# Two gate products of a transformer merge in seven block products of summed operands, with the modulation rows moved into the attention

## The chip, the cores and the metric

One Trainium2 chip, one of its cores. The metric is the device time of one execution in microseconds (us); lower is better. TensorE multiplies matrices into PSUM, VectorE and ScalarE work on elements, GpSimd here only starts accumulating DMAs, SyncE starts most of the loads.

## The reference, cut to what matters

Two layers over 512 latent tokens and 256 context tokens, 1024 channels, all in fp32. Each layer modulates a normalised input, projects it into four branches (A: dense attention, D: windowed attention, B: a Fourier mix, C: a spatial gate) and merges them:

```
def _merge(h, outs, gates, w_br, w_merge, b_merge, w_out):
    yb = jnp.stack([o * jax.nn.silu(z) for o, z in zip(outs, gates)], axis=2)
    y = jnp.einsum('bnrw,rwd->bnrd', yb, w_br)
    g = jax.nn.sigmoid(h @ w_merge + b_merge).reshape(b, n, N_BRANCH, D_MODEL)
    return jnp.sum(g * y, axis=2) @ w_out
```

The gate product `h @ w_merge` is 1024 by 1024 for each branch; the branch product `y` has a depth of 256. The modulation (shift, scale and gate of each layer, for the latent vector `c` and the context vector `c_ctx`) is `silu(c) @ w_ada + b_ada`.

## The kernel before

Everything stands transposed: channels on the 128 partitions (8 tiles `kk`), the 768 tokens in the free dimension, context in columns 0 to 255, latent in 256 to 767. Layer 0 computes all 768 columns, layer 1 the 512 latent ones.

A product keeps fp32 accuracy with two halves of each operand: `hi` is the value rounded to the matmul's type, `lo` the rest, and a product is three matmuls, hi by hi, hi by lo and lo by hi (`mm3`, line 181). The halves of the modulated input are the tiles `hh` and `hl`. Weights come in pieces of 128 x 512 or 128 x 256: `plan` (lines 136 to 151) lists them in the order of use, `wload` (154) starts their loads on SyncE's queue, at most 5 pieces ahead and with 3 buffers, `wround` (162) makes `hi` on ScalarE and `lo` on VectorE, and `wnext` (173) hands out the next piece and rounds up to the piece after it. Each of `hi` and `lo` has 3 buffers.

`merge` (line 645) does one branch in 8 tiles of 128 output channels. A tile takes two pieces of the gate's weights and one of the branch's: for the latent 512 columns and the context's 256 columns the gate product over 8 `kk` (24 matmuls each) and the branch product over 2 (6 each). Then ScalarE's tanh makes the gate (668), VectorE multiplies it with the branch product (670), and the result is added to `M` by a GpSimd DMA (676) or, in the last merge, by VectorE (674), which is followed by the rounding of `M` into `MH` and `ML` (678 to 685). The context columns' bank comes from tag `ctag`; tag "o" has one bank, "t" two, "mm" three.

The written order comes from generators that yield a cost at each step. `drive` (867) runs a main generator and lets a filler or a side generator go on as the costs allow: the attention of A and D is the main one, at a cost per unit of `PACE` (27; 48 units in layer 0), and the filler holds the projections, the merge of C and, once A's attention has ended, the merge of A (931 to 935). What is left of the filler runs after the attention (947). Then come the merge of D and the merge of B, with a side generator at `SIDE` = 0.42 (948 to 957): first `fnet` (781), the Fourier mix that the merge of B needs, then `ada_rest` (247). That one computes 24 rows of the modulation on VectorE (273), two instructions for each half row (`at`), from the vectors in `cb`; its buffers come from tags "z", "sc" and "p". In layer 1 the same with 8 rows and one vector. A planner of the framework then sets the order on each engine: an instruction whose buffer and inputs are ready may go ahead of one that is written before it. Pools have a fixed number of buffers: "k" 10, "z" 4, "yb" 8, "sc" 3, "p" 3, "q" 4.

`Rope.finish` (471) turns queries and keys with the cosine and sine tables `krope`, loaded once (404). `outp` (960) multiplies `MH` and `ML` with the output weights.

## Time and profile before

| | us |
|---|---|
| median of 3 runs | 1202.47 (1201.67 to 1204.15) |
| profiled execution: its own time | 1203.12 |
| its span | 1201.3 |
| TensorE busy / VectorE busy / ScalarE busy | 1180.7 / 734.0 / 472.6 |
| layer 0: attention | 112 to 443 |
| layer 0: last tiles of the merge of A | to 476.1 |
| layer 0: merge of D, first to last branch product | 489.6 to 565.1 |
| layer 0: merge of B, first to last branch product | 575.6 to 648.8 |

The profiled execution's time has 1.8 us around its span. [...]

### The profile page before, as it was taken

The numbers are of one execution on the slowest core, as the hardware profiler recorded it, in microseconds if no ns is written. First come the engines' busy times: TensorE is split into PE (matmuls) and PEld (weight loads), VectorE is DVE, ScalarE is ACT, GpSimd is POOL, SyncE is SP. The second block draws the span as 40 slices with busy tenths as digits, with TensorE's granted clock in tenths as the row PEclk, the third lists the DMA queues.
The fourth block names the chain that finished last, engine by engine and source line by source line (L and its number), as shares of the span: only waits on it lengthen the run. The fifth ranks groups of instructions, "written<-read, shape, count | busy, mean of one in ns | idle before, by whom it ended". The sixth has DMA issues, their size and how long they took to land. (4 is left out here: it accounts for less than half of the span.)

```text
span 1201.3 us, 18858 instructions
## 1 busy us (share of the span) xinstructions
PE 1180.7 (98%) x7164; PEld 1002.3 (83%) x7164; DVE 734.0 (61%) x1567; ACT 472.6 (39%) x935; POOL 14.4 (1%) x20
## 2 busy tenths in 40 slices
PE   6999999999999999999999999999999999999998
PEld 3789888888888888988888888887888888888887
DVE  4683557545565453577886469767756666476553
ACT  5443534433333332322333246545444444333431
POOL 0000000000000000000000000000000000000000
PEclk9999999999999999999999999999999999999999
DMA  7708113212111334567653454462322213355353
GB/s 286 264 17 212 54 45 94 57 36 61 54 45 49 80 79 120 125 180 201 192 163 101 140 161 143 133 170 89 101 63 76 65 57 90 103 171 156 97 171 123
DMA packets 76090, 138.81 MB, mean 116 GB/s; under 512 B 9056, under 2 KB 19424, under 8 KB 76000
## 3 DMA queue, kind: packets, MB, share of 16 engines
q1 hardware_dynamic: 66640, 120.30, 33.8%
q10 hardware_dynamic: 7056, 11.02, 3.1%
q0 software_dynamic: 2304, 6.29, 2.8%
q8 instruction: 56, 0.92, 0.3%
q14 instruction: 34, 0.28, 0.1%
HBM read 115.56 MB, written 4.19 MB: 100 GB/s over the span
## 5 line engine op out<-in xcount | busy, mean ns | idle before, releaser
L169 ACT CAST wh<-wr 128x512 fp32r<-128x512 f32 (+1 forms) x320 | 184.2, 577 | 362.0 <-PE gc L185 95.7
L170 DVE TENSOR_TENSOR wl<-wr,wh 128x512 fp32r<-128x512 f32 (+1 forms) x320 | 202.8, 636 | 191.5 <-ACT wh L169 189.8
L184 PE MATMUL gl<-hh,wh 128*128 128x512 f32 x512 | 204.1, 399 | 0.0
L185 PE MATMUL gl<-hl,wh 128*128 128x512 f32 x512 | 200.2, 391 | 0.0
L187 PE MATMUL gl<-hh,wl 128*128 128x512 f32 x512 | 199.9, 391 | 0.0
L187 PEld LDWEIGHTS gl<-hh,wl 128*128 128x128 f32 x512 | 96.1, 188 | 20.9
L184 PEld LDWEIGHTS gl<-hh,wh 128*128 128x128 f32 x512 | 96.5, 188 | 16.7 <-issue 0.2
L185 PEld LDWEIGHTS gl<-hl,wh 128*128 128x128 f32 x512 | 96.5, 189 | 16.2
L573 DVE TENSOR_REDUCE mx<-s 128x1 f32<-128x768 f32 (+3 forms) x80 | 61.6, 770 | 78.5 <-PE s L567 36.0
L581 ACT ACTIVATE p<-s,ng 128x768 f32<-128x768 f32 (+3 forms) x80 | 60.0, 750 | 102.1 <-DVE ng L578 58.5
L273 DVE CUSTOM_DVE_ANT_0 aj<-at,cb 128x512 f32<-128x512 f32 x112 | 74.2, 688 | 8.3 <-DMA M<-g 4.4
L184 PE MATMUL gc<-hh,wh 128*128 128x256 f32 x256 | 73.5, 287 | 0.0
L187 PE MATMUL gc<-hh,wl 128*128 128x256 f32 x256 | 72.5, 283 | 0.0
L185 PE MATMUL gc<-hl,wh 128*128 128x256 f32 x256 | 72.4, 283 | 0.0
L184 PE MATMUL p<-hh,wh 128*128 128x512 f32 (+1 forms) x192 | 71.2, 371 | 0.0
L184 PE MATMUL ow<-MH,wh 128*128 128x512 f32 (+1 forms) x200 | 69.5, 347 | 1.0 <-DVE xn L972 1.0
L187 PE MATMUL ow<-MH,wl 128*128 128x512 f32 (+1 forms) x200 | 69.4, 347 | 0.8 <-DVE wl L170 0.8
L185 PE MATMUL ow<-ML,wh 128*128 128x512 f32 (+1 forms) x200 | 69.4, 347 | 0.0
L187 PE MATMUL p<-hh,wl 128*128 128x512 f32 (+1 forms) x192 | 68.2, 355 | 0.0
L185 PE MATMUL p<-hl,wh 128*128 128x512 f32 (+1 forms) x192 | 68.2, 355 | 0.0
L668 ACT ACTIVATE g<-gl,bmh 128x512 f32<-128x512 f32 x64 | 43.8, 685 | 60.1 <-PE gl L187 42.0
L597 PE MATMUL tp<-kconst,p 128*128 128x128 f32 x368 | 53.2, 272 | 0.0
(465 smaller groups left out, 2428.3 us busy)
## 6 DMA issues: line engine op xcount, KB each, us to landing
wr<-in_wm_dram SPq DMA_DIRECT2D x128, 256.0 KB, 2.7
wr<-in_win_dram SPq DMA_DIRECT2D x72, 256.0 KB, 2.8
at<-in_wadat_dram SPq DMA_DIRECT2D x64, 256.0 KB, 3.2
wr<-in_wo_dram SPq DMA_DIRECT2D x40, 256.0 KB, 2.9
aw<-in_wada_dram SPq DMA_DIRECT2D x16, 512.0 KB, 5.7
wr<-in_wm_dram SPq DMA_DIRECT2D x64, 128.0 KB, 2.2
ks<-yk SPq DMA_DIRECT2D x32, 192.0 KB, 4.2
M<-g POOLq DMA_DIRECT2D x16, 384.0 KB, 4.9
```

Source lines behind the costliest of these rows:

```text
L169: A.copy(hi[:, :n], raw[:, :n])
L170: V.tensor_sub(lo[:, :n], raw[:, :n], hi[:, :n].bitcast(F32))
L184: T.matmul(d, wh, xh[:, c0:c1], start=first and op, stop=False)
L185: T.matmul(d, wh, xl[:, c0:c1], start=False, stop=False)
L187: T.matmul(d, wl, xh[:, c0:c1], start=False, stop=last and cl)
L273: V.tensor_tensor_reduce(out=junk[:, :512], in0=w[:, :512], in1=cb[2 * v + half][:, :512], scale=0.5, scalar=0.0, op0=ALU.mult, op1=ALU.ad ...
L573: V.reduce_max(out=mx, in_=sv, axis=AX.X)
L581: A.activation(p[:, :nk], sv, AF.Exp, bias=ng, scale=0.125, accum_out=sm_)
L597: T.transpose(tp[:, (i - g0) * P:(i - g0 + 1) * P], p[:, i * P:(i + 1) * P], ident)
L668: A.activation(g[:, q0:q1], gp, AF.Tanh, scale=0.5, bias=bmh[:, r * 8 + j:r * 8 + j + 1])
```

## The change

For the merges of D and B in layer 0 the gate product is done as a product of 2 x 2 blocks with seven block products in place of eight (the scheme of Strassen in Winograd's form). The weights of tiles j and j + 4 make the four blocks (two output tiles by two halves of the depth), and the 768 columns are split in two halves `H1`, `H2` of 384. `merged_s` lists the loads and items of such a round; `prep` makes the sums of weights on VectorE; `combos` makes the sums of columns of `hh` + `hl` and rounds them; `first_sum` puts the rounded first sum into `hh` and `hl` in place; `merge_s` runs the seven blocks and the two branch products of a round, four rounds per merge. Banks `z`, `x`, `y` hold the block products, which are added up partly in PSUM and partly in `g0`, `g1`.

Three tiles of the merge of A (of 8, `HELD` = 5 stay in the filler) are held back until the attention has ended; `fnet` and `combos` are the side work beside them. The rows of the modulation are made one half row per step with a single buffer `row`, and in both layers the steps are laced into the merge of C, `z1`, `b` and the merge of A, one per 4800 units of cost (`ADA`); what is left follows as side work. `cb` and the rope tables share two buffers (tag "rt"), and the tables are loaded again for each use, from ScalarE's queue. `wnext` rounds one piece further ahead, everywhere. Layer 0's pace is 3900.

```diff
-PACE = (4500, 4000)
+PACE = (3900, 4000)
+ADA = 4800
+HELD = 5
...
+        prt = pool("rt", 2)
+        prow = pool("row", 1)
...
+        def merged_s(l, r):
+            def a(j, h):
+                return (wm[l, r, j, :, 512 * h:512 * h + 512], 512, "wraw" if h and j < 4 else "z")
+
+            def y(j):
+                return (wm[l, r, j, :, 1024:], 256)
+
+            first = [load(*a(0, 0)), load(*a(4, 0)), load(*a(4, 1)), load(*a(0, 1))]
+            for j in range(4):
+                a11, a21, a22, a12 = first
+                y0 = load(*y(j))
+                y1 = load(*y(j + 4))
+                if j < 3:
+                    first = [load(*a(j + 1, 0)), load(*a(j + 5, 0)), load(*a(j + 5, 1)), load(*a(j + 1, 1))]
+                s1 = []
+
+                def prep(a11=a11, a12=a12, a21=a21, a22=a22, s1=s1):
+                    t = tl("p", f"s1_{a11}")[:, :512]
+                    V.tensor_add(t, raws[a21], raws[a22])
+                    V.tensor_sub(raws[a21], raws[a11], raws[a21])
+                    V.tensor_sub(raws[a11], t, raws[a11])
+                    V.tensor_sub(raws[a12], raws[a12], raws[a11])
+                    s1.append(t)
+
+                item(a11, 512)
+                item(a12, 512)
+                item(a12, 512, prep, lambda k=a11: raws[k])
+                item(a12, 512, None, lambda k=a21: raws[k])
+                item(a12, 512, None, lambda s1=s1: s1[0])
+                item(y0, 256)
+                item(y0, 512, None, lambda k=a12: raws[k])
+                item(y0, 512, None, lambda k=a22: raws[k])
+                item(y1, 256)
...
+            merged(l, R_A)
+            for r in (R_D, R_B):
+                (merged if l else merged_s)(l, r)
+            outw(l)
...
+            for k in range(len(raws), min(upto, len(loads))):
+                src, n, tag = loads[k]
+                if tag == "z":
+                    raws[k] = tl("z", f"wr{k}")[:, :512]
+                else:
+                    raws[k] = pw.tile([P, 512], F32, name=f"wr{k}", tag="wraw", bufs=W_RAW)
+                nc.sync.dma_start(raws[k][:, :n], src)
...
         def wnext():
 
             i = cnt[0]
             cnt[0] += 1
-            wload(i + LOADS)
+            wload(max(k for k, *_ in items[i:i + LOADS]))
             wround(i + 2)
+            while prepped[0] < min(i + 3, len(items)):
+                prep = items[prepped[0]][2]
+                if prep:
+                    prep()
+                prepped[0] += 1
+            wround(i + 3)
             return ready[i]
...
+            fetch(0)
+            for i, (half, l, j) in enumerate(steps):
+                if i % len(names) == 0:
+                    cb.clear()
+                    for v in range(nv):
+                        t = prt.tile([P, 512], F32, name=f"cb{v}{half}{nv}", tag="rt")
+                        nc.scalar.dma_start(t, crow[v:v + 1, half * 512:half * 512 + 512].to_broadcast([P, 512]))
+                        cb.append(t)
                     yield 1000
+                    for v, t in enumerate(cb):
+                        th = tl("sc", f"cbt{v}{half}{nv}")
+                        A.activation(th[:, :512], t, AF.Tanh, scale=0.5)
+                        V.scalar_tensor_tensor(out=t, in0=th[:, :512], scalar=1.0, in1=t, op0=ALU.add, op1=ALU.mult)
                     yield 1000
-                if j in (7, 15, 23):
+                for v in range(nv):
+                    junk = tl("sc", f"aj{l}_{j}_{half}{v}")
+                    V.tensor_tensor_reduce(
+                        out=junk[:, :512], in0=row[i], in1=cb[v], scale=0.5,
+                        scalar=0.0, op0=ALU.mult, op1=ALU.add, accum_out=macc[j // 16][:, j % 16, v, half:half + 1])
+                fetch(i + 1)
+                yield 1000
...
+            def tables(name):
+                if not TAB:
+                    for i in range(2):
+                        t = prt.tile([P, NL], F32, name=f"rt{i}{name}", tag="rt")
+                        nc.scalar.dma_start(t, krope[:, i * NL:(i + 1) * NL])
+                        TAB.append(t)
+                return TAB
...
+                    cos, sin = tables(name)
                     V.tensor_add(s[:, 0, cs], s[:, 0, cs], s[:, 1, cs])
...
-            def merge(r, first=False, final=False, ctag="mm"):
-                for j in range(KT):
+                for j in part:
...
+            HN = (WC.stop - WC.start) // 2
+            H1, H2 = slice(WC.start, WC.start + HN), slice(WC.start + HN, WC.stop)
+            BO = {}
+            def combos():
+                t23 = [[[tl("k", f"T{n}{part}{i}{l}", F32R) for i in range(2)] for part in "hl"] for n in (2, 3)]
+                t4 = [pq.tile([P, 2, NT], F32R, name=f"T4{part}{l}", tag="q") for part in "hl"]
+                t1 = [tl("k", f"T1{i}{l}") for i in range(2)]
+
+                def at(ts, kk):
+                    return [t[kk // 2][:, (kk % 2) * HN:(kk % 2) * HN + HN] for t in ts]
+
+                for n in (11, 21, 22, 1, 2, 3, 4):
+                    BO[n] = []
+                for kk in range(4):
+                    fa, fb = tl("sc", f"fa{l}{kk}"), tl("p", f"fb{l}{kk}")
+                    for f, k_ in ((fa, kk), (fb, kk + 4)):
+                        V.tensor_add(f[:, WC], hh[k_][:, WC].bitcast(F32), hl[k_][:, WC].bitcast(F32))
+                    one = at([t1], kk)[0]
+                    V.tensor_sub(one, fa[:, H2], fa[:, H1])
+                    V.tensor_sub(fa[:, H2], fb[:, H2], fa[:, H2])
+                    V.tensor_sub(fb[:, H2], fb[:, H2], one)
+                    V.tensor_sub(fb[:, H1], fb[:, H1], fb[:, H2])
...
+                    for n, (hi, lo), src in ((2, two, fb[:, H2]), (3, three, fa[:, H2]), (4, four, fb[:, H1])):
+                        A.copy(hi, src)
+                        V.tensor_sub(lo, src, hi.bitcast(F32))
+                        BO[n].append((hi, lo))
+                    BO[1].append((one, None))
...
+                    yield 4000
+
+            def first_sum():
+                for kk in range(4):
+                    src, hi, lo = BO[1][kk][0], hh[kk][:, H2], hl[kk][:, H2]
+                    A.copy(hi, src)
+                    V.tensor_sub(lo, src, hi.bitcast(F32))
+                    BO[1][kk] = (hi, lo)
+
+            def block(dst, n, start):
+                wh, wl = wnext()
+                for i, (xh, xl) in enumerate(BO[n]):
+                    q = slice(i * P, (i + 1) * P)
+                    T.matmul(dst, wh[:, q], xh, start=start and i == 0, stop=False, skip_group_check=True)
+                    T.matmul(dst, wh[:, q], xl, start=False, stop=False, skip_group_check=True)
+                    T.matmul(dst, wl[:, q], xh, start=False, stop=i == 3, skip_group_check=True)
+                    yield 1.27 * HN
...
+            def merge_s(r, final=False):
+                for j in range(4):
+                    z, x, y = (bank(f"{n}{l}{r}{j}")[:, :HN] for n in "zxy")
+                    g0, g1 = (tl("sc", f"g{l}{r}{i}") for i in (j, j + 4))
+                    def gate(i, jj, g, yd):
...
+                    yield from block(z, 11, True)
+                    A.copy(g0[:, H1], z)
+                    yield from block(x, 21, True)
+                    V.tensor_add(g0[:, H1], x, g0[:, H1])
+                    A.activation(g0[:, H1], g0[:, H1], AF.Tanh, scale=0.5, bias=bias[0])
+                    yield from block(z, 2, False)
+                    A.copy(g1[:, H1], z)
+                    yield from block(y, 3, True)
+                    yield from block(z, 1, False)
+                    A.copy(g1[:, H2], z)
+                    V.tensor_add(g1[:, H2], y, g1[:, H2])
+                    yd = yield from branch(r, j, ("o", "t"))
+                    yield from block(z, 22, False)
+                    A.activation(g0[:, H2], z, AF.Tanh, scale=0.5, bias=bias[0])
+                    gate(0, j, g0, yd)
+                    yield from block(y, 4, False)
+                    V.tensor_add(g1[:, H1], y, g1[:, H1])
+                    A.activation(g1[:, WC], g1[:, WC], AF.Tanh, scale=0.5, bias=bias[1])
+                    yd = yield from branch(r, j + 4, ("t", "o"))
+                    gate(1, j + 4, g1, yd)
+                    if final:
...
+                            hi = tl(("yb", "k", "p", "k")[j], f"MH{l}{jj}", F32R)
+                            lo = lq[:, i, :] if j else tl("yb", f"ML{l}{jj}", F32R)
+                            A.activation(hi[:, WC], M[jj][:, WC], AF.Copy, scale=0.5)
+                            V.scalar_tensor_tensor(out=lo[:, WC], in0=M[jj][:, WC], scalar=0.5,
+                                                   in1=hi[:, WC].bitcast(F32), op0=ALU.mult, op1=ALU.subtract)
+                            MH[jj], ML[jj] = hi, lo
...
+            def laced(main, other, per):
+
+                bal = 0
+                for x in main:
+                    yield x
+                    bal += x or 0
+                    if bal >= per:
+                        bal -= per
+                        next(other, None)
...
+            if not last:
+                ada = ada_rest([(0, j) for j in range(16, 24)] + [(1, j) for j in range(16)])
+            own = HELD if l == 0 else KT
...
+                ("mc", lambda: laced(merge(R_C, first=True), ada, ADA)), ("z1", lambda: laced(zblock(1), ada, ADA)),
+                ("b", lambda: laced(bproj(), ada, ADA)),
+                ("ma", ("a0", lambda: laced(merge(R_A, part=range(own)), ada, ADA))),
...
+            side = seq([("fnet", fnet)] + ([("sums", combos)] if l == 0 else []) + [("ada", lambda: ada)])
+            if l == 0:
+                drive(paced(merge(R_A, ctag="o", part=range(own, KT)), 1.0), side)
+                while "sums" not in flags:
+                    next(side)
+                first_sum()
+                drive(paced(merge_s(R_D), SIDE), side)
+                drive(paced(merge_s(R_B, final=True), SIDE), side)
...
-            xn = [tl("yb", f"xn{i}") for i in range(KT)]
+            xn = [tl("yb" if i < 4 else "z", f"xn{i}") for i in range(KT)]
```

## Rows read from the trace of the kernel before

**Rows 1.** The page, part 1: busy us, share of the span, instructions.

```profile
PE 1180.7 (98%) x7164; PEld 1002.3 (83%) x7164; DVE 734.0 (61%) x1567; ACT 472.6 (39%) x935; POOL 14.4 (1%) x20
```

**Rows 2.** Windows by stage: PE, PEld, DVE, ACT, POOL busy; PEclk, DMA share, GB/s.

```profile
112.00:443.50 331.50, 331.50 (x2287) 287.31 (x2286) 185.31 (x415) 131.50 (x289) 3.91 (x4) 1.00 0.23 62
443.50:476.10 32.60, 32.60 (x195) 28.46 (x194) 11.12 (x23) 8.82 (x17) 2.58 (x3) 1.00 0.45 110
476.10:502.50 26.40, 26.40 (x175) 23.97 (x174) 12.83 (x44) 7.82 (x15) 1.72 (x2) 1.00 0.50 121
498.00:565.00 67.00, 67.00 (x387) 59.05 (x386) 49.51 (x131) 20.77 (x38) 5.16 (x6) 1.00 0.72 189
575.60:648.80 73.20, 73.20 (x422) 64.53 (x421) 61.53 (x152) 24.96 (x43) 0.00 (x0) 1.00 0.49 148
585.00:627.00 42.00, 42.00 (x244) 37.05 (x243) 37.83 (x95) 14.39 (x25) 0.00 (x0) 1.00 0.54 163
```

**Rows 3.** Timeline of PE: start, duration; first tiles of D, a tile of B.

```profile
476.08 0.40 PE L184 MATMUL gl<-hh,wh 128*128 128x512 f32 x1
...
491.75 0.40 PE L184 MATMUL gl<-hh,wh 128*128 128x512 f32 x1
...
586.06 0.40 PE L184 MATMUL yl<-yb300h,wh 128*128 128x512 f32 x1
...
588.16 0.40 PE L184 MATMUL gl<-hh,wh 128*128 128x512 f32 x1
...
590.91 0.28 PE L184 MATMUL gc<-hh,wh 128*128 128x256 f32 x1
...
592.34 0.40 PE L184 MATMUL gl<-hh,wh 128*128 128x512 f32 x1
...
596.52 0.40 PE L184 MATMUL yl<-yb300h,wh 128*128 128x512 f32 x1
```

**Rows 4.** Timeline of DVE in the merge of B: start, duration.

```profile
589.44 0.68 DVE L273 CUSTOM_DVE_ANT_0 aj<-at,cb 128x512 f32<-128x512 f32 x1
590.05 0.08 DVE L273 DVE_READ_ACCUMULATOR2_ANT macc<- 128x1 f32 x1
590.05 0.95 DVE L674 TENSOR_TENSOR M<-M,g 128x768 f32<-128x768 f32 x1
590.92 0.42 DVE L170 TENSOR_TENSOR wl<-wr,wh 128x256 fp32r<-128x256 f32 x1
591.25 0.69 DVE L273 CUSTOM_DVE_ANT_0 aj<-at,cb 128x512 f32<-128x512 f32 x1
```

**Rows 5.** Instructions on tile yl: ns min/median/max, first and last start.

```profile
L184 PE MATMUL yl<-yb100h,wh x8: 396/396/396, 489.6 to 565.1; 128*128 128x512 f32 x8
L184 PE MATMUL yl<-yb300h,wh x8: 396/396/396, 575.6 to 648.8; 128*128 128x512 f32 x8
```

**Rows 6.** Instructions on tiles kd and tab, same columns.

```profile
L791 PE MATMUL gcs<-wf,kd x4: 273/274/377, 479.1 to 479.8; 128*128 128x128 f32 x4
...
L784 ACTq DMA_DIRECT2D kd<-in_kdft_dram x1: 334/334/334, 449.0 to 449.0; - x1
...
L824 ACTq DMA_DIRECT2D tab<-in_dfl_dram x1: 334/334/334, 452.0 to 452.0; - x1
L824 ACTq DMA_DIRECT2D tab<-in_dfc_dram x1: 334/334/334, 453.2 to 453.2; - x1
```

**Rows 7.** Windows, columns as in Rows 2: the start and three idle places.

```profile
0.00:25.00 25.00, 14.11 (x60) 6.37 (x60) 13.31 (x32) 14.78 (x23) 0.20 (x4) 0.93 0.94 338
...
87.00:90.00 3.00, 1.60 (x7) 0.60 (x5) 3.00 (x5) 2.22 (x6) 0.00 (x0) 1.00 0.34 58
90.00:94.00 4.00, 4.00 (x12) 3.20 (x12) 4.00 (x6) 1.57 (x2) 0.00 (x0) 0.58 0.91 245
...
800.00:825.00 25.00, 23.05 (x131) 18.16 (x130) 21.55 (x40) 10.92 (x21) 0.00 (x0) 1.00 0.42 110
```

**Rows 8.** The page, part 6: DMA issues, count, KB each, us to landing.

```profile
wr<-in_win_dram SPq DMA_DIRECT2D x72, 256.0 KB, 2.8
at<-in_wadat_dram SPq DMA_DIRECT2D x64, 256.0 KB, 3.2
```

**Rows 9.** Groups of ACT by form: busy us, mean ns, idle before.

```profile
L169 ACT CAST wh<-wr 128x512 fp32r<-128x512 f32 x256 | 158.5, 620 | 310.6 <-PE gl L185 82.3 <-PE gc L185 58.1 <-issue 49.5
...
L601 ACT COPY pt<-tp 128x384 f32<-128x384 f32 x32 | 15.3, 478 | 8.5 <-PE tp L597 8.3
```

**Rows 10.** Instructions on tile krope: first and last start.

```profile
L404 SPq DMA_DIRECT2D krope<-in_krope_dram x1: 422/422/422, 36.1 to 36.1; - x1
```

**Rows 11.** Groups of PE by form, 87 to 90 us.

```profile
L184 PE MATMUL p_cu<-hh,wh 128*128 128x512 f32 x2 | 0.9, 446 | 0.6 <-ACT wh L169 0.6
```

**Rows 12.** Timeline of ACT in the merge of B: one tile's two tanh.

```profile
605.75 0.69 ACT L668 ACTIVATE g<-gl,bmh 128x512 f32<-128x512 f32 x1 [2.20 <-DVE wl L170]
...
609.52 0.47 ACT L668 ACTIVATE g<-gc,bmh 128x256 f32<-128x256 f32 x1
```

More of the change, by code (lines that the diff above doesn't have):

```diff
@@ L264, in ada_rest @@
[L264 to L277 removed]
+            steps = [(half, l, j) for half in range(2) for l, j in names]
@@ L282, in ada_rest @@
                                     op=ALU.add)
-                if j == 15:
+                if half and j == 15:
                     mk_a(l, slice(0, 8))
```

136 lines of the change are left out of this document (70 added, 66 removed).

## Prediction

> **What bounds the kernel now.** I read the busy line first: TensorE computes for 1180.7 of a span of 1201.3 us [rows 1]. The windows by stage then show where: the attention of layer 0, the rest of the merge of branch A, and the merges of D and B have TensorE at work in every microsecond at a granted clock of 1.00, with VectorE at 56%, 34%, 74% and 84% [rows 2]; in the 42 us from 585 to 627 VectorE is at 90% and TensorE still never waits. So here the number of matmul columns sets the end, and an instruction of VectorE or ScalarE costs nothing until its engine is late. The change takes columns out of these two merges and gives VectorE more to do ahead of them: the question is whether VectorE stays on time.
>
> **Block products (taken out).** A tile of the merge of B takes 10.46 us (586.06 to 596.52); a run of 12 gate matmuls of 512 columns 2.75 us (0.229 each), one of 12 of 256 columns 1.43 us (0.119 each) [rows 3]. Two tiles now need 4 x (2.75 + 1.43) = 16.72 us for their gates. The new round for two tiles has 7 blocks x 4 x 3 = 84 matmuls of 384 columns. No run of that shape stands in the trace; scaled by columns it costs 0.172 from the row of 512 and 0.179 from that of 256, and I take the mean of the two intervals, 0.174: 14.62 us a round. The branch products stay. Gain 2.1 us a round, 8 rounds in the two merges: **16.7 us** (13.5 to 18.2).
>
> **Column sums beside the three held tiles.** VectorE's starts follow one another by 0.61 us after an instruction of 512 columns, 0.87 after 768, 0.33 after 256 [rows 4]; 384 is put halfway, 0.47. The sums need 4 x (2 of 768 + 7 of 384) = 4 x 5.03 = 20.1 us of VectorE. Beside them run `fnet` and the tiles themselves. A tile's own share is 3 roundings and 2 gates, 3 x 0.61 + 2 x 0.33 = 2.49. For `fnet`: the first tile of the merge of D took 15.67 us instead of 10.46 and the later seven 75.5 instead of 73.2 [rows 3, 5], so its TensorE part is 7.5 us; the window 476.1 to 502.5 has 12.83 us of VectorE, of which (26.4 - 7.5) / 10.46 x 2.49 = 4.5 are the tiles', so its VectorE part is 8.3 [rows 2]. The held stage lasts 3 x 10.46 + 7.5 = 38.9 us on TensorE.
>
> Could the sums start sooner? VectorE has 21 us free from 443.5 to 476.1 [rows 2], and transfers are hoisted to where a buffer is free: `kd` was issued at 449.0, the two `tab` at 452.0 and 453.2, 26 us ahead of the first matmul that reads `kd` at 479.1 [rows 6]. But these three hold all buffers of tag "p", and each `fb` of the sums needs one, so the sums begin only when `fnet`'s first matmuls have run, inside the held stage. I put 2.5 us of idle VectorE before that.
>
> By the costs that the generators yield, a tile has 1.27 x 768 x 10 = 9,754 units and `fnet` 880 + 1,720 + 1,715 + 860 + 858 = 6,033; each of the four groups of sums yields 4,000. At pace 1.0 the fourth group is emitted at 6,033 + 12,000 = 18,033 of the 29,261 units of the three tiles. The gates of the second held tile come behind it, and the third tile's context bank (tag "o" has one) waits for them: due 2 x 10.46 + 2.75 + 7.5 = 31.2 us into the stage. In front lie 8.3 + 20.1 + two tiles' gates 1.9 + six roundings 3.1 + idle 2.5 = 35.9. **Wait 4.7 us.** The next date, the third block of the first round at 43.1, needs 6.5 more of roundings, sums of weights and gates and some 3 of modulation rows: 45.4, which the 4.7 already covers. Bounds: 0 if the planner finds the idle time; 12 if all eight row steps emitted there (1.22 each) go first.
>
> Such a wait can also cost clock. [...] From 800 to 825 an idle of 1.95 us in all left the clock at 1.00. I take the first row: **1.7 us** (0 to 3.4). [...]
>
> **The new rounds themselves.** A round is 14.62 + 2 x 2.09 = 18.8 us. VectorE: 7 x 0.61 + 2 x 0.33 of rounding, 4 x 0.61 of weight sums, three additions of 0.47, four gate instructions 1.9: 10.7, and 14.1 in the merge of B, which has four more of 768. What is left of the modulation rows is 17 steps, each held to a transfer of 3.2 us [rows 8] because the buffer is single: at most four a round, 5 us. That is 84% of a round in D, 75% in B without rows and 102% with them for the little that may be left; 90% was harmless [rows 2]. Bank z is emptied three times a round by ScalarE with one block (2.09 us) of cover; a copy of 384 columns takes 0.48 and a weight cast in front of it 0.62 [rows 9]. **1 us** over all rounds (0 to 3).
>
> **Modulation rows during the attention.** One step per 4,800 units of merge C, `z1`, `b` and five tiles of merge A makes 16 + 3 + 6 + 10 = 35 of 52. VectorE there: 185 busy, plus 35 x 1.22 = 43, less 7.5 for the held tiles, in 331 - 31 us: 74%, below what was harmless. Cost 0, covered by VectorE's slack; up to 5 if four steps in 35 stand in front of a softmax that TensorE needs next. The tighter pace (3900 for 4500, 48 units) only takes out what the held tiles took from the filler. SyncE's queue now waits for a row's buffer ahead of weight loads: they landed 2.8 us after issue [rows 8] and are asked for two pieces (over 8 us) ahead: 0.
>
> **Other edits.** The rope tables were issued at 36.1 us [rows 10]; now they hang on no slot and can go out within the first 25 us, when the DMA engines are at 0.94 [rows 7]. 512 KB at 338 GB/s is 1.6 us; I take **0.8** (0 to 1.6). Weights are rounded one piece further ahead everywhere: waits for ScalarE's cast like the 0.6 us near 89 [rows 11] can shrink, **-0.5** (-3 to 0). Layer 1's rows move the same way; TensorE had no idle there, 0.
>
> **Sum.** 1203.1 (the profiled execution) - 16.7 + 4.7 + 1.7 + 1.0 + 0.8 - 0.5 = 1194.1; the median of the runs is 0.65 lower, so **1193.5 us**.
>
> **Rivals.**
> All covered: the sums go into the idle time before the held tiles. For it: 21 us free there, and an order that is not the written one: the activation of the context columns is written first, and ScalarE ran that of the latent columns 3.8 us sooner [rows 12]. Against: the "p" buffers. 1202.5 - 16.7 = **1186 us**.
> The gain is eaten: the wait is at its bound of 12 and the clock at 3.4: 1202.5 - 16.7 + 15.4 + 1.3 = **1202.5 us**, no change.
> Slower: VectorE keeps the written order at each round's end. Then the last gates (0.94; in the merge of B also 0.87 + 2 x 0.87), the four weight sums 2.44, the rounding 0.61 and, in D, a row step or two of 1.22 stand in line for the third block, which is due 2 x 2.09 + 0.35 = 4.5 us into the round. The excess is about 1.3 us a round in D, 2.05 in B: 13.4, and with the clock's 1.7 in half the rounds 20. 1202.5 - 16.7 + 20 + 6.4 = **1212 us**. It decides from 1.1 us a round on (16.7 - 7.7 = 9.0, over 8). For it: the line is really that long. Against: [rows 12], and 90% without a wait.
>
> **How the numbers follow.** Likeliest (0.45): partly covered, 1193.5, its own range 1189 to 1199. All covered 0.23 (1184 to 1189). Eaten 0.15 (1199 to 1206). Slower by the rounds 0.17 (1206 to 1216). A measurement here can tell 0.2%, 2.4 us. Faster: 0.45 + 0.23 + a fifth of the third, 0.71; same 0.10; slower 0.19. The range 1185 to 1206 leaves out a little of the second case and most of the last.
>
> **What would show it.** Right: runs of 12 matmuls of 384 columns at about 2.09 us; rounds of 18.8; TensorE waiting on VectorE some 5 us in one place, near the end of branch A's merge, with a dip of the clock behind it; the attention without waits. Wrong: waits on `z` or on a rounded weight in every round (the slower rival), instructions of the sums before the first matmul of `fnet` (the covered one), a start that is later by over 2 us, or waits for softmax rows in the attention.

## The result and the profile after

The changed kernel takes **1248.1 us** (median, 1245.1 to 1250.0) against 1202.5 before: ratio 1.038, 95% interval 1.0363 to 1.0396. The forecast was 1193.5, between 1185 and 1206, and faster. The profiled execution has a span of 1248.2 us.

The page, part 1, of the changed kernel:

```profile
PE 1182.2 (95%) x7068; PEld 1008.8 (81%) x7068; DVE 796.1 (64%) x1687; ACT 499.3 (40%) x991; POOL 14.1 (1%) x20
```

TensorE has 96 matmuls fewer than in [rows 1], and yet works 1.5 us longer; its idle time grew from 20.6 to 66.0 us. So something stands still, and something else runs slower. The windows of 25 us around the end of branch A's merge show both (columns as in [rows 2]):

```profile
475.00:500.00 25.00, 21.43 (x123) 18.26 (x121) 24.57 (x50) 12.78 (x25) 1.72 (x2) 1.00 0.38 88
500.00:525.00 25.00, 1.49 (x6) 1.29 (x5) 15.45 (x38) 2.19 (x4) 0.00 (x0) 0.61 0.35 105
525.00:550.00 25.00, 20.90 (x96) 19.34 (x95) 14.98 (x39) 6.36 (x13) 1.72 (x2) 0.78 0.40 103
550.00:575.00 25.00, 17.43 (x71) 15.31 (x70) 13.81 (x35) 5.48 (x10) 0.86 (x1) 0.77 0.55 150
575.00:600.00 25.00, 24.82 (x137) 23.61 (x137) 14.22 (x26) 10.70 (x20) 2.14 (x3) 0.96 0.37 90
600.00:625.00 25.00, 25.00 (x147) 24.30 (x146) 15.48 (x28) 11.44 (x21) 3.02 (x4) 1.00 0.52 118
```

In [rows 2] TensorE was at work in each of these microseconds, at a clock of 1.00. Now from 500 to 525 it works for 1.49 us of 25, and the following 50 us run at a clock of 0.77 to 0.78. From 575 on it is nearly as before. VectorE is full only in the first of these windows (24.57 of 25). What TensorE waits for (view of waits: us in total, times, longest):

```profile
PE x L811 <- ACT g L742: 23.5, 1, 23.5
...
PE z L811 <- ACT g L841: 5.8, 2, 3.0
...
PE gl L248 <- DVE wl L225: 1.7, 1, 1.7
...
PE gc L245 <- DVE g L744: 1.4, 1, 1.4
```

One wait of 23.5 us, ahead of the second block (`x`) of the first round of D, for ScalarE's tanh of line 742: the gate of the last held tile, whose bank the block needs. ScalarE's timeline (start, duration, in brackets the idle time before and what ended it) hands the question on:

```profile
506.94 1.14 ACT L224 CAST wh<-wr 128x512 fp32r<-128x512 f32 x2 [8.44 <-DVE wr L173]
522.61 0.47 ACT L742 ACTIVATE g<-gc,bmh 128x256 f32<-128x256 f32 x1 [14.54 <-DVE macc L339]
```

The tanh waits 14.54 us for VectorE's accumulator read of a **modulation-row step**. The tanh writes a buffer of tag `sc`, and of these there are three; the junk products of the row steps (the element products, of which only the accumulated sum is used) had them. VectorE's timeline shows why so long:

```profile
509.08 0.69 DVE L339 CUSTOM_DVE_ANT_0 aj<-at,cb 128x512 f32<-128x512 f32 x1 [0.20 <-DMA at<-in_wadat_dram]
...
513.39 0.69 DVE L339 CUSTOM_DVE_ANT_0 aj<-at,cb 128x512 f32<-128x512 f32 x1 [0.21 <-DMA at<-in_wadat_dram]
...
517.27 0.69 DVE L339 CUSTOM_DVE_ANT_0 aj<-at,cb 128x512 f32<-128x512 f32 x1 [2.57 <-DMA at<-in_wadat_dram]
...
521.26 0.69 DVE L339 CUSTOM_DVE_ANT_0 aj<-at,cb 128x512 f32<-128x512 f32 x1 [2.68 <-DMA at<-in_wadat_dram]
...
526.45 0.42 DVE L744 SCALAR_TENSOR_TENSOR g<-g,gc 128x256 f32<-128x256 f32 x1
```

The first product of each step starts about 4 us after that of the step before (513.39, 517.27, 521.26), and ahead of it VectorE idles up to 2.7 us for the row `at`: one buffer, so a row is fetched only when the one before it is used up. The work of a step is 1.22 us. Eight steps are emitted ahead of the gate, at 496.22, 500.56, 504.99, 509.08 and so on to 525.22; the tanh gets its buffer when the seventh has ended, and VectorE's part of the gate comes behind the eighth, at 526.45. SyncE's queue in the same stretch (start, time from first to last issue):

```profile
510.43 24.47 SPq L320 DMA_DIRECT2D at<-in_wadat_dram  x7
```

Seven row fetches one behind the other, each waiting for the buffer, with the weight loads of the next round behind them. The starts of the second block of the eight rounds, by TensorE's timeline, are 523.7, 551.9, 584.8, 603.6, 622.4, 641.2, 660.0 and 678.8: two long rounds of 28.2 and 32.9 us, where steps and late weights still interfere, and from the third on **18.80 us** each, the forecast's 18.8. The run of 12 matmuls of 384 columns is there too (first matmul of block `x`, and of the block behind it):

```profile
551.87 0.33 PE L811 MATMUL x<-hh,wh 128*128 128x384 f32 x1
...
553.95 0.33 PE L811 MATMUL y<-T3h,wh 128*128 128x384 f32 x1
```

2.08 us for the run (2.09 forecast): a matmul is shown with 0.33 us, but the next starts 0.17 us behind it. The clock behind the long wait, in windows from its end on:

```profile
523.70:530.00 6.30, 4.21 (x12) 3.70 (x12) 2.82 (x7) 0.00 (x0) 0.86 (x1) 0.50 0.40 109
530.00:537.00 7.00, 6.27 (x22) 6.27 (x23) 3.89 (x13) 2.02 (x4) 0.00 (x0) 0.56 0.48 113
537.00:545.00 8.00, 6.71 (x36) 5.84 (x35) 4.57 (x12) 2.40 (x5) 0.00 (x0) 1.00 0.40 117
```

The granted clock was 0.50 and 0.56 in the first two windows and 1.00 in the third. Another such stretch lies between 560 and 580 (0.67 from 560 to 570, 0.65 from 570 to 580). In the window at 0.50 the matmuls of block `x` are shown with 0.52 us and start 0.32 us apart, against the 0.33 and 0.17 above. So TensorE's busy time did not fall although it has fewer columns: in no_rows below, with the same 7068 matmuls, it is 1169.0 us, 13.2 less.

### The profile page after: what moved, and what is told of

Read it like the earlier page. It is cut to its first block, busy times and chain, and to the rows that moved or that the text cites. A ratio compares the mean times of both kernels' runs of the same rounds, so it can differ in the third digit from the quotient of the medians.

```text
span 1248.2 us, 18881 instructions
## 1 busy us (share of the span) xinstructions
PE 1182.2 (95%) x7068; PEld 1008.8 (81%) x7068; DVE 796.1 (64%) x1687; ACT 499.3 (40%) x991; POOL 14.1 (1%) x20
## 4 chain that ended last, share of the span: by engine, by line
PE 86%; DVE 6%; DMA 4%; ACT 2%; issue 2%; SPq 0%; ACTq 0%; DVEq 0%
PE gl L245 7%; PE gl L248 7%; PE gl L246 7%; PE o L704 4%; PE tp L671 3%; PE p L245 3%; PE p L246 3%; PE p L248 3%; PE ow L246 3%; PE ow L245 3%; PE ow L248 3%; PE yl L245 2%; PE yl L248 2%; PE yl L246 2%; PE z L811 2%
## 5 line engine op out<-in xcount | busy, mean ns | idle before, releaser
L245 PE MATMUL gl<-hh,wh 128*128 128x512 f32 x384 | 154.2, 402 | 0.0
L248 PE MATMUL gl<-hh,wl 128*128 128x512 f32 x384 | 150.5, 392 | 1.7 <-DVE wl L225 1.7
L246 PE MATMUL gl<-hl,wh 128*128 128x512 f32 x384 | 150.1, 391 | 0.0
L248 PEld LDWEIGHTS gl<-hh,wl 128*128 128x128 f32 x384 | 72.2, 188 | 17.7 <-DVE wl L225 2.1
L245 PEld LDWEIGHTS gl<-hh,wh 128*128 128x128 f32 x384 | 72.4, 189 | 12.9 <-ACT g L742 0.2
L246 PEld LDWEIGHTS gl<-hl,wh 128*128 128x128 f32 x384 | 72.5, 189 | 12.6
L704 PEld LDWEIGHTS o<-pt,vt 128*64 128x64 f32 x736 | 40.9, 136 | 17.2 <-issue 13.3
L704 PE MATMUL o<-pt,vt 128*64 128x128 f32 x736 | 52.5, 279 | 1.0 <-DVE pt L673 1.0
L671 PEld LDWEIGHTS tp<-kconst,p 128*128 128x128 f32 x368 | 44.6, 140 | 11.0 <-issue 0.9
L673 DVE COPY pt<-tp 128x384 f32<-128x384 f32 (+1 forms) x80 | 41.9, 524 | 8.9 <-PE tp L671 8.9
```

What stands on the lines that cost most here:

```text
L245: T.matmul(d, wh, xh[:, c0:c1], start=first and op, stop=False)
L246: T.matmul(d, wh, xl[:, c0:c1], start=False, stop=False)
L248: T.matmul(d, wl, xh[:, c0:c1], start=False, stop=last and cl)
L671: T.transpose(tp[:, (i - g0) * P:(i - g0 + 1) * P], p[:, i * P:(i + 1) * P], ident)
L673: V.tensor_copy(pt[:, g0 * P:g1 * P], tp[:, :(g1 - g0) * P])
L704: T.matmul(dst[64 * hx:64 * hx + 64, :], vt[kt_ // 3][:, kt_ % 3, c0:c0 + 64], pts[hx][:, j * P:(j + 1) * P], start=(j == 0), stop=(j == l ...
```

## The experiments

Three times in each trace divide a run: the first score product of the attention (`s`), the first block of D (`z`), the first output product (`ow`). For the kernel before, the second is put at 476.1 + 7.5 = 483.6, since `fnet`'s 7.5 us now come earlier. The views of tiles `z` and `ow` of the changed kernel (ns, first and last start):

```profile
L811 PE MATMUL z<-hh,wh x96: 331/335/690, 497.2 to 693.2; 128*128 128x384 f32 x96
```

```profile
L245 PE MATMUL ow<-MH,wh x200: 277/389/397, 697.9 to 1244.3; 128*128 128x512 f32 x60, 128*128 128x256 f32 x40
```

| run | median us | ratio (95%) | `s` | `z` | `ow` | `z` to `ow` | span |
|---|---|---|---|---|---|---|---|
| before | 1202.5 | | 114.8 | 483.6 | 650.9 | 167.3 | 1201.3 |
| after | 1248.1 | 1.038 (1.036 to 1.040) | 116.0 | 497.2 | 697.9 | 200.7 | 1248.2 |
| junk_psum | 1217.9 | 1.013 (1.011 to 1.016) | 116.1 | 495.8 | 667.2 | 171.4 | 1217.6 |
| no_fetch | 1217.8 | 1.013 (1.011 to 1.015) | 116.7 | 497.0 | 667.4 | 170.4 | 1217.1 |
| junk_psum_all | 1217.1 | 1.013 (1.010 to 1.015) | 115.0 | 496.0 | 663.8 | 167.8 | 1215.1 |
| spread | 1212.2 | 1.009 (1.007 to 1.011) | 115.3 | 495.6 | 661.1 | 165.5 | 1209.4 |
| rows_in_attention | 1216.2 | 1.012 (1.010 to 1.014) | 117.3 | 504.6 | 664.6 | 160.0 | 1215.8 |
| rows_in_outp | 1216.7 | 1.013 (1.011 to 1.014) | 116.2 | 497.0 | 664.7 | 167.7 | 1214.5 |
| no_rows | 1204.1 | 1.002 (1.001 to 1.003) | 113.3 | 491.0 | 650.6 | 159.6 | 1202.9 |
| no_rows_held4 | 1198.1 | 0.997 (0.996 to 0.998) | 113.0 | 486.4 | 644.3 | 157.9 | 1195.8 |
| no_rows_held4_p | 1195.1 | 0.995 (0.993 to 0.996) | 113.4 | 486.4 | 641.1 | 154.7 | 1192.6 |
| no_rows_pool | 1208.1 | 1.005 (1.003 to 1.007) | 115.3 | 498.1 | 656.0 | 157.9 | 1206.4 |
| best_c | 1210.7 | 1.007 (1.005 to 1.009) | 115.7 | 492.9 | 660.4 | 167.5 | 1210.6 |
| best_e | 1272.3 | 1.058 (1.057 to 1.060) | 116.7 | 490.3 | 646.2 | 155.9 | 1273.0 |

From `ow` to the end it is 548 to 552 us in all of them but best_e. Eight rounds of 18.8 are 150.4.

**Is it the row steps, and by what? (junk_psum, no_fetch, junk_psum_all)** The first run gives the junk product another home:

```diff
+two = pps.tile([P, 1024], F32, name=f"ajs{l}_{j}_{half}", tag="s") if nv == 2 and i >= 35 else None
 for v in range(nv):
-    junk = tl("sc", f"aj{l}_{j}_{half}{v}")
+    junk = two[:, 512 * v:512 * v + 512] if two else tl("sc", f"aj{l}_{j}_{half}{v}")
```

> The 17 row steps that are left after the attention write their junk product to a bank of PSUM (tag s) instead of a buffer of tag sc. Buffer theory (the junk tiles take the three sc buffers ahead of the gate of held tile 7, and each is given back only when a row of 4 us has landed): the wait of 23.5 us falls below 8, the span to 1212 to 1226, since the steps still stand in VectorE's order with their own waits for rows. VectorE overload theory (too many additions in the held stage): nothing changes, 1245. Round theory (the seven blocks hand over too slowly): the 23.5 shrinks but the waits come back in each round, over 1235.

The second leaves the transfers out:

```diff
 def fetch(i):
-    if i < len(steps):
+    if nv == 2 and i >= 35:
+        row.append(row[34])
+    elif i < len(steps):
```

> The last 17 row steps fetch nothing and read the row that is already there, so part of the modulation rows is computed from wrong data; VectorE's instructions, their junk tiles in sc and their places in the order are the same. Row transfer theory: a step takes 1.3 us instead of 4, the wait of 23.5 falls to 0 to 6 and the time to 1198 to 1210. VectorE overload theory: same VectorE work, same wait, 1240 to 1248. Round theory: 1235 or more.

Both edits reached less than meant. The generator of the rows stops 52 times, but 4 of the stops are for the condition vectors: there are 48 steps, 31 run in the attention, and the index 35 spares the first four of the 17 left over. The wait of block `x` in junk_psum, and in no_fetch:

```profile
PE x L812 <- ACT g L743: 8.9, 1, 8.9
```

```profile
PE x L813 <- ACT g L744: 14.8, 1, 14.8
```

8.9 and 14.8 us of 23.5. In no_fetch the junk tiles and VectorE's work are the same; of the seven steps that the tanh waits for, three lose their transfer: 8.7 us less, about 3 x (4.0 - 1.2) = 8.4. In junk_psum VectorE's part of the gate now stands right behind the fourth step, the last that still uses `sc`. VectorE has the same work in both as before, and the wait fell: the overload theory fails. The third run reaches all 17 (index 31):

> Run junk_psum with the junk product of all 17 left-over row steps in PSUM; there the first four (rows 23, 0, 1, 2) still took buffers of sc, as in no_fetch the first four still fetched, so the two runs took away only part of what they were to take away. Here the gate of held tile 7 stands behind one row step in VectorE's order. Buffer theory: the wait of block x falls from 23.5 (8.9 in junk_psum) to under 3.5, total 1207 to 1213, with the steps still in the rounds. If something else holds that gate: 6 us or more stay, 1216 or more.

```profile
PE z L812 <- ACT wh L224: 8.8, 2, 6.9
...
PE gc L245 <- DVE g L745: 1.4, 1, 1.4
```

No wait for that gate is left: **the `sc` buffers held it**. The time expected (1207 to 1213) was missed, because 6.9 us appear one block later, at the third block's weights. VectorE's timeline has three row steps there, 3.7 us, among the splits, first sums and weight sums that this block needs; without any row the same wait is 3.6 (below), 3.3 less. So the second wait goes with what stands in VectorE's line ahead of these weights.

**Where may a step stand? (spread, rows_in_attention, rows_in_outp)**

```diff
-side = seq([("fnet", fnet)] + ([("sums", combos)] if l == 0 else []) + [("ada", lambda: ada)])
+side = seq([("fnet", fnet)] + ([("sums", combos)] if l == 0 else []) + ([("ada", lambda: ada)] if l else []))
...
-    drive(paced(merge_s(R_D), SIDE), side)
-    drive(paced(merge_s(R_B, final=True), SIDE), side)
+    run(laced(merge_s(R_D), ada, 6000))
+    run(laced(merge_s(R_B, final=True), ada, 6000))
+    run(ada)
```

> No row step during the held tiles; the 17 left over go one per 6000 units of the merges of D and B. Buffer and row transfer theory: the stretch from the first block of D to the first output product is 150 to 156 us instead of 200.7, total 1198 to 1205 (13.6 us of later start before the block products stay). VectorE overload theory: the column sums still crowd the held stage, wait of 10 us or more there, 1215 to 1235. Round theory: 1230 or more.

1212.2, 36 us less than the changed kernel, but 7 above what was expected: `z` to `ow` is 165.5, not 150 to 156. The 23.5 is gone.

```diff
-ADA = 4800
+ADA = 3200
```

> One row step per 3200 units instead of 4800, so all 52 fall into the attention. Row theories: the merges of D and B take 150 to 153 us, the attention gets a little later (17 more steps, by the 12 us that 35 cost about 3 to 6 us), total 1199 to 1206. VectorE overload theory: 1215 or more with the wait in the held stage. If the attention cannot bear the steps: softmax waits of over 15 us in all, 1215 or more with clean rounds.

1216.2, above the 1199 to 1206 of the row theories and in the time of the last case (1215 or more), though not by its mechanism: the waits for the softmax come to 2.5 us, not 15. Behind the first round the rounds are as forecast; two windows of one round each (the merge of D, and of B):

```profile
543.40:562.20 18.80, 18.80 (x110) 18.27 (x109) 11.36 (x20) 8.34 (x15) 1.72 (x2) 1.00 0.46 112
...
600.00:619.00 19.00, 19.00 (x111) 18.47 (x110) 14.55 (x24) 9.71 (x18) 0.00 (x0) 1.00 0.24 72
```

TensorE never waits there. But `z` comes at 504.6 instead of 497.2: the steps are paid for before it. From `s` to `z` it takes 387.3 us, against 381.2 in the changed kernel; how the steps bring that about is open.

> The changed kernel with only some four of the 17 left-over row steps emitted in the rounds of D and B and the rest beside the output products, their junk in PSUM. If a left-over step costs only where it stands in a round: 1204.1 without rows plus the rows of the attention (5 by the start of the first block, 496 against 491), 1207 to 1210. If the steps are placed into the rounds all the same or cost as much beside the output products: 1211 to 1214.

The edit is that of junk_psum_all, and the steps are handed out beside `outp` (in D one per 25000 units, in B one per 60000). 1216.7, above both expectations. The view of the junk tile (ns; first and last start) has all 17 left-over steps, two products each, inside the rounds:

```profile
L340 DVE CUSTOM_DVE_ANT_0 ajs<-at,cb x34: 692/699/702, 503.5 to 587.3; 128x512 f32<-128x512 f32 x34
```

An order of emission is not an order of execution: where nothing holds a step back, it is placed earlier. So this run could not tell what a step costs beside the output products.

**What do the block products give without any row? (no_rows, no_rows_held4, no_rows_held4_p, no_rows_pool)**

```diff
 def ada_rest(names, nv=2):
+    if nv == 2:
+        V.memset(mods[0][:, 16:24, :], 0.0)
+        V.memset(mods[1][:, 0:16, :], 0.0)
+        mk_a(1, slice(0, 8))
+        return
```

> The changed kernel without layer 0's 52 row steps: no fetch, no product; what they give is set to zero, so the third modulation part of layer 0 and two parts of layer 1 are left out. The first block of D started at 497.2, by the kernel before it would have been 483.6. If the rows of the attention cost that (SyncE's queue and VectorE's order in front of the softmax): first block at 487 to 490, total 1189 to 1196. If the new pace and the held tiles cost it: still 493 to 497, total 1199 to 1206. The rounds themselves: 150 to 156 in either case.

`z` at 491.0, between the two expectations, and 1204.1, in the range of the second: **without a single row step in layer 0 the kernel is no faster than the one before**. From `z` to `ow` it takes 159.6 instead of 150.4, above the 150 to 156 expected. The waits, and the windows of the held stage's last 31 us and of the first round:

```profile
PE z L816 <- ACT wh L224: 5.5, 2, 3.6
...
PE gl L248 <- DVE wl L225: 1.7, 1, 1.7
...
PE gc L245 <- DVE g L749: 1.4, 1, 1.4
```

```profile
460.00:491.00 31.00, 27.93 (x164) 24.15 (x163) 29.52 (x71) 14.70 (x31) 1.72 (x2) 1.00 0.34 77
491.00:510.00 19.00, 15.38 (x72) 14.57 (x72) 13.21 (x23) 6.88 (x13) 0.86 (x1) 0.82 0.40 104
```

VectorE is at 29.52 of 31 us, so the forecast's mechanism is there: 1.7 + 1.4 us in the held stage, then 3.6 ahead of the third block of the first round (the 5.5 holds another 1.9 in the last round), and a clock of 0.82 over 19 us, at most 3.4 us lost. Four held tiles with slower handing out give VectorE more time:

```diff
-HELD = 5
+HELD = 4
...
-drive(paced(merge(R_A, ctag="o", part=range(own, KT)), 1.0), side)
+drive(paced(merge(R_A, ctag="o", part=range(own, KT)), 0.6), side)
```

> Run no_rows with four tiles held back and the work beside them handed out at 0.6 of its pace, so that the sums spread over all four (in spread_held4 they still stood ahead of the first two gates). VectorE theory: waits in the held stage under 1, first round's wait under 1.5, total 1195 to 1199. Rival of the z buffers: held stage clean, but 3 us remain ahead of the third block, 1200 to 1203. Rival of the attention: softmax waits grow by 4 or more, 1203 to 1208.

```profile
PE z L816 <- DVE wr L174: 3.1, 1, 3.1
```

`z` at 486.4, 4.6 earlier, and 1198.1, faster than before (ratio 0.997) and in the range of the VectorE theory. The held stage has no wait left; the first round keeps 3.1, as the z-buffer rival had it, though here for the weight sum itself. So one weight of that round goes to another buffer:

```diff
-"wraw" if h and j < 4 else "z"
+"wraw" if h and j < 4 else "p" if h and j == 4 and r == R_D else "z"
...
-if tag == "z":
-    raws[k] = tl("z", f"wr{k}")[:, :512]
+if tag in "zp":
+    raws[k] = tl(tag, f"wr{k}")[:, :512]
```

> Run no_rows_held4 (layer 0's row steps left out) with one weight piece of the first round of D loaded into a buffer of tag p instead of z. There TensorE waited 3.1 us ahead of the third block for a weight sum. z buffer theory (two of the four z buffers hold fnet's result until the last held product is through, so the third weight of the first round is fetched late): the wait falls under 1, total 1193 to 1196. Rival (VectorE's line of splits and sums is as long by itself): the wait stays, 1197 to 1199.

```profile
PE z L816 <- ACT wh L224: 1.9, 1, 1.9
```

Only the last round's 1.9 is left of all waits for `z`: 1195.1. VectorE's line and the z buffers had been two limits, one right behind the other; the buffer alone, with five tiles in the filler, was not run. The other cure was to take work off VectorE:

```diff
-V.tensor_add(f[:, WC], hh[k_][:, WC].bitcast(F32), hl[k_][:, WC].bitcast(F32))
+G.tensor_add(f[:, WC], hh[k_][:, WC].bitcast(F32), hl[k_][:, WC].bitcast(F32))
```

> Run no_rows (layer 0's row steps left out) with the eight additions of 768 columns of the column sums on GpSimd instead of VectorE: 7 of the sums' 20 us leave VectorE. VectorE theory of the held stage: its waits of 1.7, 1.4 and 3.6 and the half clock behind them go down to under 3 in all, 1204.1 becomes 1195 to 1200. Rival (the first round waits for buffers of tag z, which fnet's two tiles hold until the last held product is through): the 3.6 stays, 1200 to 1203. Rival (GpSimd is so slow at it that the sums end later): 1206 or more.

1208.1, slower: `z` at 498.1 instead of 491.0, although 7 us of work left VectorE. Of the 7.1 us, 2.0 lie before the first score product; 1.9 are longer waits in the held stage (5.0 for rounded weights, in place of 1.7 + 1.4), and a clock of 0.91 over the 38.1 us from 460 on costs up to 3.4. What happened on VectorE stands in the last section.

**Small terms, on top of spread (spread_tables, spread_round2, spread_held4).** 

> Run spread with the rope tables issued on SyncE's queue behind the stack weights, as in the kernel before. Table theory (512 KB among the first transfers delays the start): the last stack product starts at 65.7 instead of 67.7, and the time falls by 1.2 to 2.5 from 1212. Rival (the delay is swallowed by the waits of the norm and of the first projection): start moves, time within 0.5 of 1212.

1212.1, no change, as the rival had it. The start moved by more than was expected (last stack product at 64.0 instead of 67.7) and `z` came 3.6 us earlier (492.0), but in this trace the stretch from `ow` to the end, which the edit does not touch, took 551.7 us instead of 548.3.

> Run spread with weights rounded two pieces ahead, as in the kernel before, not three. My step in the prediction (rounding further ahead can only shorten waits for casts): 1213 to 1222, with more waits of z on wh and wl in each round. Rival (three ahead means that every cast stands in ScalarE's and VectorE's order waiting for the one buffer that TensorE is still reading, and holds back the softmax and gates behind it): 1203 to 1209, the first block of D earlier than 493.

1213.7, 1.5 above spread and at the lower end of the first expectation; the rival's 1203 to 1209 did not come. `z` starts at 490.3, earlier than 493 as the rival said, but TensorE's timeline shows that this is only a change of order:

```profile
490.61 0.34 PE L811 MATMUL z<-hl,wh 128*128 128x384 f32 x1
491.11 0.50 PE L247 MATMUL gl<-hh,wl 128*128 128x512 f32 x1 [0.17 <-DVE wl L225]
...
496.34 0.34 PE L812 MATMUL z<-hh,wl 128*128 128x384 f32 x1
```

Two matmuls of the block went ahead of the last 30 of the held tile, and the block goes on at 496.3; in spread it starts at 495.6, behind all of them. So the 169.6 from `z` to `ow` is no price of the rounds either.

> Run spread with four tiles of branch A held back instead of three, so the column sums have 10.5 us more of TensorE beside them. VectorE theory of the held stage: the waits there and ahead of the first round (1.7, 1.4 and 3.6) go, time 1204 to 1208. Rival (the attention misses the fifth tile as filler): softmax waits grow by 5 to 10 us, 1212 to 1220.

1212.0, no change: the sums, emitted at pace 1.0, stood ahead of the first two gates (waits of 1.2 and 1.4 stayed, and 3.2 at the first round). This is what the pace of 0.6 above mended.

**With all rows, a version that beats both? (best_a, best_b, best_c, best_e, best_e7)** 

> All row steps are done, nothing is left out: branch rows of layer 0 during the attention at one per 7600 units, those of layer 1 beside the rounds of D and B with their junk product in PSUM, rope tables on SyncE's queue, four held tiles at pace 0.6. If rows, held stage and tables are the three causes, each at the size found so far: 1204.1 without rows, less 5 for the held stage, less 1 to 3 for the tables, plus 2 for the rows of the attention and 2 to 5 for those of the rounds: 1198 to 1204, about the kernel before. If steps in a round cost as much as in run spread (0.35 us each): 1206 to 1212.

> Run best_a with the eight additions of the column sums on GpSimd as well. If VectorE is still what the held stage waits for: 2 to 4 below best_a; if four tiles were cover enough: within 1.5 of it; if GpSimd's additions come late: above it.

1215.2, above both expectations, and 1219.3, the case of the late additions. The steps beside the rounds made `z` to `ow` 178.5 us in best_a.

> All rows done: four held tiles at pace 0.6, the p buffer for the first round, left-over steps beside the output products with junk in PSUM, some seven of them in the rounds. By the parts: 1198.1 less 3 for the p buffer, plus 4 to 5 for the rows of the attention, plus 0 to 2 for the others: 1198 to 1202. If rows and the narrow rounds add up worse than one by one: 1204 to 1210.

1210.7, the case in which rows and narrow rounds add up worse. The left-over steps were placed from 524.9 to 632.5, inside the rounds again, and TensorE waits there for gates and weights:

```profile
PE yc L245 <- DVE g L834: 4.2, 3, 1.7
PE z L812 <- ACT wh L224: 3.1, 1, 3.1
```

best_e holds the late steps back by a dependence, a copy of one column of the last merge tile into the row's buffer ahead of its fetch:

```diff
+if late and nv == 2:
+    w = tl("p", f"at{l}_{j}_{half}{nv}")[:, :512]
+    V.tensor_copy(w[:, :1], late[0][:, :1].bitcast(F32))
```

> All rows done, nothing left out. Four held tiles at pace 0.6 and the p buffer as in no_rows_held4_p (1195.1 without rows); some 22 row steps during the attention, none in the held stage or the rounds of D and B, 26 beside the output products, kept there by a copy of one column of the last merge tile into the row's buffer ahead of its fetch (in rows_in_outp and best_c the steps were placed into the rounds although they were emitted behind them). If a step costs where it stands in a round (0.6 us in best_c) and 0.1 to 0.3 in the attention, and nothing beside the output products: 1195 plus 3 to 6, 1197 to 1201, faster than the kernel before or even. If a step costs wherever it stands: 1206 or more.

```profile
PE n1a L415 <- DVE ones1a L408: 54.8, 1, 54.8
PE ow L246 <- DVE xn L1187: 17.6, 1, 17.6
```

1272.3. Up to `ow` it is ahead of all above that do all rows (646.2; the rounds take 155.9, and from `s` to `z` its 22 steps cost 0.6 us against no_rows_held4_p, 373.6 to 373.0). But beside the output products the steps come one per 4 to 7 us, with the fetch behind the copy and the copy behind VectorE's other work, and layer 1's norm, placed behind the last of them on VectorE, makes TensorE wait 54.8 us. VectorE's timeline there:

```profile
778.24 0.70 DVE L345 CUSTOM_DVE_ANT_0 ajs<-at,cb 128x512 f32<-128x512 f32 x1
778.86 0.14 DVE L345 DVE_READ_ACCUMULATOR2_ANT macc<- 128x1 f32 x1
779.19 0.17 DVE L408 MEMSET ones1a<- 128x128 f32 x1
```

With 32 late steps it is worse still:

> Run best_e with some 16 row steps in the attention and 32 beside the output products. If the output products hide them: 1 to 2 below best_e. If VectorE has no room for so many there, layer 1's norm waits for its rows: 3 to 12 above best_e, with a wait of TensorE behind the last output products.

1299.4, 27 above best_e where 3 to 12 was expected, though `ow` comes earlier (641.5). Fetches of best_e on SyncE's queue near the end, six in 23 us:

```profile
734.10 23.01 SPq L325 DMA_DIRECT2D at<-in_wadat_dram  x6
```

So no kernel that computes all rows came below 1202.5. A second buffer for the rows, so that one is fetched while the one before it is used, was not run.

## Why the prediction was wrong

**The step that failed** is the one on the rows that are left: "17 steps, each held to a transfer of 3.2 us because the buffer is single: at most four a round, 5 us". Everything in it was seen, the single buffer, the transfer and the number, but a step was priced as 1.22 us of VectorE alone. Each of its two junk tiles takes one of the three `sc` buffers, and a step comes only every 4 us, since each waits for the next row; and the gate of the last held tile needs one of these buffers and is emitted behind eight steps. Even the upper bound of the wait, 12 us "if all eight row steps emitted there (1.22 each) go first", has the right steps and the wrong price: the seven that the tanh had to wait for took VectorE from 496.2 to 522.6 us, 26.4, where 7 x 1.22 is 8.5. By the table, the left-over rows cost 200.7 - 159.6 = **41 us** between `z` and `ow`. Above eight clean rounds (150.4) the changed kernel has 50.3 there: 23.5 of the wait, 23.5 of the two long rounds with the low clock in them (0.50 to 0.67), and 3.3 elsewhere; the kernel without rows has 9.2.

**Modulation rows in the attention**, put at 0 to 5: `z` at 497.2 against 491.0 without rows, so **6.2**, of which 2.7 arise before the first score product, which moves by 2.0 between two kernels without rows (no_rows and no_rows_pool), and 3.5 behind it; 48 steps there (rows_in_attention) cost 13.6, 4.0 of it before that point. The forecast counted 35 of 52 steps; the generator's stops include four without a step, so it was 31 of 48, and the 17 that are left came out right by luck. "Below what was harmless" went by VectorE's share, but TensorE waited 2.7 us for the softmax (1.0 without rows, none in the kernel before); 22 steps, at wider spacing, cost 0.6 behind that point.

**Block products**, -16.7: right. The run of 384 columns takes 2.08 us and the round 18.80, eight of them 16.9 less than the 167.3 of the kernel before; the clean rounds show no wait on VectorE's line at the round's end, so the slower rival of the forecast did not come. **The new rounds themselves**, +1.0 (0 to 3): the wait of 1.9 for a rounded weight in the last round, which even the run with both repairs has, and up to 1.7 of clock behind it (0.92 over the last 21.1 us), 3.6 in all.

**Wait beside the column sums**, +4.7 with bounds 0 and 12: the mechanism was right, the sums did not start before `fnet`'s first products, and VectorE was full. The size was off: 3.1 in the held stage and 3.6 ahead of the third block of the first round. The forecast had this second date as one "which the 4.7 already covers"; it left out of VectorE's line the four late splits of the first sums (1.96 us) and did not see that two of the z buffers come free only with `fnet`'s last split. With both mended, 159.6 becomes 154.7 and the stage before it 4.6 shorter.

**Clock**, +1.7 (0 to 3.4): the 1.7 was the author's estimate from one place before, 4 us at 0.58 [rows 7], or 4 x 0.42; no run shows this term. What the runs showed in its place is at most 3.4 in the first round of no_rows and at most 13 us in the changed kernel (6.2 from 523.7 to 537, 6.8 from 550 to 600, by the windows above). There the clock was 0.50 and 0.56 in the 13.3 us behind the wait of 23.5 us, and 1.00 in the 8 us after them. For a short wait its length alone does not tell what it costs. The 3.1 in no_rows_held4 cost little more than itself: `z` to `ow` is 157.9 there and 154.7 in no_rows_held4_p without it. And the wait of 1.9 in the last round left a clock of 1.00 in no_rows and 0.65 in no_rows_held4_p (windows behind it, in this order):

```profile
635.60:640.00 4.40, 4.38 (x24) 4.02 (x25) 2.81 (x6) 2.31 (x5) 0.00 (x0) 1.00 0.15 12
626.10:630.00 3.90, 3.90 (x17) 3.90 (x17) 1.33 (x4) 0.82 (x3) 0.00 (x0) 0.65 0.00 0
```

**Rope tables**, +0.8: not settled. The first score product lies between 111.6 and 117.3 in these runs and moves with edits that do not touch it. **Rounding further ahead**, -0.5: two pieces instead of three gave 1213.7 against 1212.2, in the direction of the forecast and too small to tell. **Layer 1**: from `ow` to the end 550.3, before 550.4, as said.

The sum by the runs: 1248.2 - 45.3 for the rows (no_rows) - 10.3 for the held stage and the first round (no_rows_held4_p) = 1192.6, a median of 1195.1, near the 1193.5 that was forecast. But that kernel leaves the rows out and has both repairs, and that it meets the number is luck: its wait beside the column sums is gone, where the forecast had 4.7 and 1.7 for it. It gains 12.6 us from `z` to `ow`, not 16.7, and loses 4.2 from `s` to `z` (373.0 against 368.8 in the kernel before), where the forecast had nothing. Of the 4.2 us 1.7 are waits; no run shows where the rest comes from.

## What to carry to other kernels

A step of background work is priced by what it holds, and how long, not by the time that it computes: count the rotating buffers that it takes, who else draws from them, and the transfer that decides when it gives them back. Work handed out "beside" a stage runs where the order of each engine puts it, and that order need not be the written one: look for it in the trace, and hold it by data only where a late arrival hurts no one. Where two limits lie one behind the other (here VectorE's line and the z buffers), one cure leaves the wait of the other standing (3.1 us in no_rows_held4, until the buffer was changed too), so look for the next wait before judging the first cure.

## What the runs showed of the hardware

GpSimd's additions in no_rows_pool took 1.81 to 3.50 us for 768 columns, where VectorE took 0.95 in no_rows, and some VectorE instructions beside them took longer than elsewhere. GpSimd's timeline (start, duration), then VectorE's:

```profile
466.27 1.85 POOL L787 TENSOR_TENSOR fb<-hh,hl 128x768 f32<-128x768 f32 x1 [4.96 <-PE df L1019]
...
478.67 2.02 POOL L787 TENSOR_TENSOR fb<-hh,hl 128x768 f32<-128x768 f32 x1
```

```profile
466.62 1.53 DVE L1039 COPY yf<-ev 128x2 f32<-128x2 f32 x1
...
470.32 0.15 DVE L1039 COPY yf<-ev 128x2 f32<-128x2 f32 x1
470.39 0.55 DVE L789 TENSOR_TENSOR T<-fa 128x384 f32<-128x384 f32 x1
...
478.91 2.20 DVE L789 TENSOR_TENSOR T<-fa 128x384 f32<-128x384 f32 x1
```

The copy of 2 columns at 466.62 lasts 1.53 us and ends as GpSimd's addition (466.27 + 1.85) ends; the same copy at 470.32, with GpSimd idle, takes 0.15. The subtraction at 478.91 takes 2.20 us instead of the 0.55 of 470.39, and ends 0.42 after GpSimd's addition (478.67 + 2.02). No run shows why. More came back than had been freed: from `s` to `z` VectorE is busy for 225.6 us, against 221.8 in no_rows, although 7 us of additions had left it.
